# Eleven up-projection pairs of the second FFN as seven block products instead of eight

## The chip, the core and the metric

The kernel runs on one core of a Trainium2 chip. The metric is the device time of one launch in microseconds; the time of a kernel is the median of its runs. A core has five engines with queues of their own, each worked off strictly in order: TensorE (PE; its weight loads are PEld), VectorE (DVE), ScalarE (ACT), GpSimd (POOL) and SyncE (SP). Transfers are issued from SP's and POOL's queues. Engines wait for each other, and for transfers, on semaphores.

## What is computed

Two layers of a decoder trunk with 512 tokens, 16 meta tokens ahead of them (L = 528), a width of 1024 and an FFN width of 2816:

```python
for l in range(DEPTH):                      # DEPTH = 2
    h = mixer_sublayer(h, ...)              # attention, conformer conv and short conv groups
    h = ffn_sublayer(h, ...)
return h[:, N_META:]

def ffn_sublayer(h, pre_g, post_g, w_up, conv_w, w_down):
    u = rms_norm(h, pre_g)
    z = jnp.einsum("bld,df->blf", u, w_up)
    z = causal_depthwise_conv(z, conv_w)    # 3 taps
    g, up = jnp.split(z, 2, axis=-1)
    y = jnp.einsum("blf,fd->bld", jax.nn.silu(g) * up, w_down)
    return h + rms_norm(y, post_g)
```

Everything is float32.

## The kernel before

Channels lie on the 128 partitions, tokens along the free axis; a [1024, 528] activation is eight tiles of 128 x 528. A float32 product is made of three products in a rounded format: operands are split into a high part (a cast on ScalarE) and a low part (the rest, a subtraction on VectorE), and `mm3` (L706) issues high x high, high x low and low x high for every 128 rows k and every half of the tokens.

Weights lie in DRAM in the order of their use, in chunks of up to 128 x 1024. Each is loaded by SP into one of three `raw` buffers, cast into `whi` and subtracted into `wlo`. `next_w` hands out the next chunk and prepares two ahead; in the mixers and at the seams a planner (`Flow`) sets the order by hand, in the FFN loops the program order and a list scheduler do, on the simulated readiness of each instruction.

The FFN runs in three parts of 8, 7 and 7 pairs (`PARTS`). A pair f is a gate tile f and an up tile 22 + f of 128 channels. For each of the two, eight k, three products and two token halves are accumulated in a pair of PSUM banks (48 matmuls), VectorE multiplies the result by the token norm `rz` into one of four z buffers (`scaled`, L1988, its products on L1992 and L1995), and `ffn_gate` (L2031) applies the three taps, SiLU and the product and splits g into `yhi` and `ylo`. The input u is so far not normalised; `uhi` and `ulo` hold h times the gain. After each part eight down products add up in `yp`. The last layer needs only 514 columns of z (250 and 264 in the two halves) and 512 of the output.

GpSimd does little: memsets of constants and padding at the start; in each mixer memsets of `cxp`, `vals`, `fx`, `k` and `q`, then `dm` (L1483) and the causal selects of the probabilities (L1526). In the first layer's FFN it also issues twelve transfers `w_split` (L545), which store split weights of the second layer. Transfers issued by POOL share eight completion semaphores (lanes, DMASW0 to DMASW7): each waits for the one that last used its lane, that is the one eight before it.

Of the kernel before, what the change touches and what calls it, by code (L numbers as in the profile page):

```python
# [2 lines left out]

# [6 lines left out]
F32 = mybir.dt.float32  # L10
F32R = mybir.dt.float32r
# [4 lines left out]
P = 128  # L16
D = 1024
KD = D // P
L = 528
# [6 lines left out]
DFF = 2816  # L26
NF = DFF // P
PARTS = (8, 7, 7)
AHEAD = 2
CHUNK = 1056  # L30

# [77 lines left out]
def chunk_cols(c):  # L109
    return sum(n for _, n in c[4])  # L110
# [269 lines left out]
def tile_hybrid_trunk(ctx: ExitStack, tc: tile.TileContext, xT, wflat, pv_d, out):  # L380
# [80 lines left out]
    def const_col(name, val):  # L461
        t = T(const, [P, 1], F32, name)
        nc.gpsimd.memset(t, val)
        return t

    c_one = const_col("c_one", 1.0)
    c_eps = {RMS_EPS: const_col("c_rms", RMS_EPS), LN_EPS: const_col("c_ln", LN_EPS)}

    EXPSET = "natural_log_exp_and_others"
    nc.scalar.preload_act_table_set(EXPSET)  # L470
# [33 lines left out]
    wx = [None]  # L504


    pw_place = [None]

    def wtile(i, tag):
# [4 lines left out]
            return pw_place[0][:, :n] if tag == "whi" else pw_place[0][:, n:2 * n]  # L514
        return T(wx[0], [P, WCHUNK], F32R, tag) if i in wide else T(wp, [P, CHUNK], F32R, tag)

    def prep_one():
        i = wpos[0]
        if i >= len(chunks):
            return  # L520
# [6 lines left out]
        nc.scalar.copy(hi[:, :sz], raw[:, :sz])  # L527
        nc.vector.tensor_sub(lo[:, :sz], raw[:, :sz], hi[:, :sz].bitcast(F32))  # L528
        ready.append((i, tuple(t[:, :sz].rearrange("p (k n) -> p k n", n=n) for t in (hi, lo))))
# [1344 lines left out]
    wxs = wide_pool("wx0")  # L1874
# [77 lines left out]
    for l in range(DEPTH):  # L1952
# [14 lines left out]

        with ms, tc.manual_schedule(engines=every):
            flow.yields = YM
            y, y_at, early = mixer(l, ypool, first, wxs.close, i_spans, front, rzs, u_at)  # L1970
        ms, front, u_at = ExitStack(), None, {}
        wxs = wide_pool(f"wy{l}", [early.slot[hf] for hf in range(2)], early.third)

        with tc.tile_pool(name=f"fp{l}", bufs=2, reuse_waits="tile") as fp:
            hp = wxs.enter_context(tc.tile_pool(name=f"hg{l}", bufs=1, side="right", reuse_waits="tile"))
            rz, yp = T(hp, [P, L], F32, "rz"), T(hp, [P, KD, L], F32, "yp")

            def u_in(b, k, hf):
# [1 line left out]
                return (uhi, ulo)[b][:, k, a:z]  # L1980


            zs = [T(fp, [P, 2 + L], F32, f"z{i}", 1) for i in range(4)]
            if off:
                for t in zs:
                    nc.gpsimd.memset(t[:, :off], 0.0)
# [45 lines left out]
            def ffn_gate(f):  # L2032
# [15 lines left out]
                nc.vector.tensor_sub(glo, cs[0], ghi.bitcast(F32))  # L2048
                return ghi, glo

            g = {}
            f0 = 0
            for part, nf in enumerate(PARTS):
                for f in range(f0, f0 + nf):
                    for i in (2 * f, 2 * f + 1):
# [6 lines left out]
                        ps = mmt()  # L2062
                        mm3({hf: ps[:, hf, :iws[hf]] for hf in range(2)}, w, range(KD), u_in)
                        scaled(i, [ps[:, :, :H]] if i0 == 0 else [ps[:, hf, :iws[hf]] for hf in range(2)])
                    g[f] = ffn_gate(f)
                ks = list(range(nf))
                grhs = lambda b, k, hf, f0=f0: g[f0 + k][b][:, fw * hf:fw * (hf + 1)]
                if part < len(PARTS) - 1:
                    for m in range(KD):
                        w = next_w()  # L2070
                        ps = mmt()
                        if final:

                            mm3({0: ps[:, 0, :2 * fw]}, w, ks, lambda b, k, hf, f0=f0: g[f0 + k][b][:, :2 * fw])
                            d, src = yp[:, m, t0:], ps[:, 0, :2 * fw]
                        else:
                            mm3({hf: ps[:, hf, :fw] for hf in range(2)}, w, ks, grhs)
                            d, src = two(yp[:, m, t0:]), ps[:, :, :fw]
                        if part == 0:
                            nc.scalar.copy(d, src)  # L2080
                        else:
                            nc.vector.tensor_add(d, d, src)  # L2082
                        if l == 0 and m%2:
                            store_one()
                else:
                    gpre = None if final else pvs[l + 1][1][:, _COLS["mix_pre_g"]:]
                    first = raw = rzs = None
                    if not final:
                        raw = [[g[f0 + k][b] for k in range(nf)] + [T(ypool, [P, L], F32R, f"y{n}{nf}")] for b, n in enumerate(("hi", "lo"))]
                        raw = [[[t[:, half_sl(hf)] for t in ts] for ts in raw] if hf < 2 else None for hf in range(2)]  # L2090
                        rzs = [rz[:, half_sl(hf)] if raw[hf] else None for hf in range(2)]
                        first = First(lambda b, k, hf, raw=raw: raw[hf][b][k] if raw[hf] else u_rhs(b, k, hf), [H, H], {})
                    with tc.manual_schedule(engines=every):
                        plan_begins()
                        norms.factors([rs, zs[0][:, 2:]], h=APART)
                        flow.yields = YE
                        if not final:
                            plan_w(after_down, WE)
                        plan_w(len(chunks) if final else after_mixer[l + 1])
                        t_last = [Tok(flow.now + 7.5)]  # L2100
                        finish(norms, h, {}, o_spans, ks, grhs, lambda k, nf=nf: t_last if k == nf - 1 else [], yp,
                               gains("ffn_post_g"), gpre, SPLIT["ffn_w_down"], first, raw=raw, rzs=rzs, u_at=u_at)
                f0 += nf
        if final:
            wxs.close()


# [47 lines left out]
```

## Time and profile before

| | us |
|---|---|
| three runs | 1293.91, 1294.2, 1294.4; median 1294.2 |
| span of the profiled execution | 1292.0 (2.2 less than the median of the runs) |
| TensorE busy | 1274.1 (99%) |
| VectorE busy | 864.3 (67%) |
| ScalarE busy | 618.1 (48%) |
| GpSimd busy | 103.1 (8%) |

The first mixer runs from the start to about 215 us. In the second layer's FFN the down product of part 0 begins at about 994 us, that of part 1 at about 1117, and the last up pair ends at about 1237. A busy time is a share over stages with different limits; what bounds a stage is read from the row of that stage, and from the chain of waits, which follows the last instruction back to what released it. In a row of the groups the columns are line, engine, operation, output and inputs, shapes, count, then busy us and mean ns of one, then idle time just before and what ended it.

### The profile page before, as it was taken

What the parts mean: (1) busy time and instruction counts of PE and PEld (TensorE: products, weight loads), DVE (VectorE), ACT (ScalarE), POOL (GpSimd) and SP (SyncE); (2) the same over time, 40 slices, a digit from 0 to 9 for tenths busy, and PEclk for the clock granted to TensorE, in tenths of its full rate; (3) what the DMA queues carried; (4) which work ended last, traced back from release to release, by engine and by line L of the source; (5) the groups of instructions that cost most, each with busy time, mean ns of one, the idle gap of its engine ahead of it and who ended that gap; (6) DMA issues with size and microseconds to landing.
All of it is one profiled execution on the core that took longest, in us unless ns stands there. A gap on an engine that the chain in (4) does not pass through costs nothing. (4 is left out here: it accounts for less than half of the span.)

```text
span 1292.0 us, 24062 instructions
## 1 busy us (share of the span) xinstructions
PE 1274.1 (99%) x9802; PEld 1223.7 (95%) x9802; DVE 864.3 (67%) x1477; ACT 618.1 (48%) x1157; POOL 103.1 (8%) x266
## 2 busy tenths in 40 slices
PE   8999999999999999999999999999999999999997
PEld 8999899999999999999999998899999799989997
DVE  7888775687634664567688877757776257637664
ACT  7255577654433342334672555865543333313443
POOL 1313311000000000000003232100000000000000
PEclk9999999999999999999999999999999999999999
DMA  7136133502273225223541452344132332232221
GB/s 239 34 101 159 50 100 103 178 18 98 89 235 134 99 87 179 95 96 101 177 170 36 113 144 62 89 135 129 34 99 82 98 98 84 72 123 85 90 72 65
DMA packets 50094, 137.35 MB, mean 106 GB/s; under 512 B 6000, under 2 KB 16368, under 8 KB 49984
## 3 DMA queue, kind: packets, MB, share of 16 engines
q1 hardware_dynamic: 48208, 129.39, 32.0%
q0 software_dynamic: 1776, 6.42, 1.3%
q8 instruction: 77, 1.26, 0.4%
q14 instruction: 33, 0.27, 0.1%
HBM read 114.33 MB, written 10.62 MB: 97 GB/s over the span
## 5 line engine op out<-in xcount | busy, mean ns | idle before, releaser
L712 PE MATMUL psum<-uhi,whi 128*128 128x264 f32 (+1 forms) x1840 | 426.0, 287 | 1.6 <-ACT uhi L1927 0.8
L712 PE MATMUL psum<-ulo,whi 128*128 128x264 f32 (+1 forms) x1840 | 420.8, 284 | 0.6 <-DVE ulo L1929 0.4
L712 PE MATMUL psum<-uhi,wlo 128*128 128x264 f32 (+1 forms) x1840 | 418.8, 283 | 0.0
L712 PEld LDWEIGHTS psum<-uhi,whi 128*128 128x128 f32 x1840 | 304.9, 188 | 6.1 <-issue 1.6
L712 PEld LDWEIGHTS psum<-ulo,whi 128*128 128x128 f32 x1840 | 305.9, 189 | 1.4 <-DVE ulo L1929 0.6
L712 PEld LDWEIGHTS psum<-uhi,wlo 128*128 128x128 f32 x1840 | 305.6, 189 | 0.0
L712 PE MATMUL psum<-yhi,whi 128*128 128x264 f32 (+3 forms) x984 | 275.8, 301 | 2.4 <-ACT yp L2080 1.0
L712 PE MATMUL psum<-yhi,wlo 128*128 128x264 f32 (+3 forms) x984 | 272.9, 297 | 1.1 <-DVE wlo L668 1.1
L712 PE MATMUL psum<-ylo,whi 128*128 128x264 f32 (+3 forms) x984 | 272.3, 297 | 0.0
L527 ACT CAST whi<-raw 128x1024 fp32r<-128x1024 f32 (+1 forms) x110 | 113.2, 1031 | 195.8 <-PE psum L712 186.4
L712 PEld LDWEIGHTS psum<-yhi,whi 128*128 128x128 f32 x984 | 177.0, 188 | 10.4 <-ACT yp L2080 1.6
L712 PEld LDWEIGHTS psum<-yhi,wlo 128*128 128x128 f32 x984 | 177.3, 188 | 6.8 <-DVE wlo L668 1.5
L712 PEld LDWEIGHTS psum<-ylo,whi 128*128 128x128 f32 x984 | 177.4, 188 | 5.5
L528 DVE TENSOR_TENSOR wlo<-raw,whi 128x1024 fp32r<-128x1024 f32 (+1 forms) x110 | 131.9, 1200 | 67.7 <-ACT whi L527 65.6
L2029 DVE SCALAR_TENSOR_TENSOR c<-z,pv,c 128x528 f32<-128x528 f32 (+1 forms) x176 | 131.9, 756 | 2.7
L668 DVE TENSOR_TENSOR wlo<-raw,whi 128x1024 fp32r<-128x1024 f32 (+2 forms) x80 | 95.5, 1203 | 30.1 <-ACT whi L664 29.6
L664 ACT CAST whi<-raw 128x1024 fp32r<-128x1024 f32 (+2 forms) x80 | 81.8, 1030 | 25.6 <-PE psum L712 17.9
L1028 DVE SCALAR_TENSOR_TENSOR cacc<-apad,pv,cacc 128x528 f32<-128x528 f32 x120 | 87.6, 771 | 0.1
L2047 ACT CAST yhi<-c 128x528 fp32r<-128x528 f32 (+1 forms) x44 | 27.6, 627 | 108.8 <-DVE c L2043 108.7
L2039 ACT ACTIVATE c<-c 128x528 f32<-128x528 f32 (+1 forms) x44 | 28.1, 639 | 79.4 <-DVE c L2029 79.4
L1992 DVE TENSOR_TENSOR z<-psum,rz 128x528 f32<-128x528 f32 x40 | 28.3, 708 | 53.7 <-PE psum L712 52.2
L2027 ACT ACTIVATE c<-z,pv 128x528 f32<-128x528 f32 (+1 forms) x88 | 63.4, 727 | 0.1
(221 smaller groups left out, 1455.9 us busy)
## 6 DMA issues: line engine op xcount, KB each, us to landing
raw<-in_w_dram SPq DMA_DIRECT2D x160, 512.0 KB
raw<-in_w_dram SPq DMA_DIRECT2D x32, 448.0 KB
h<-in_x_dram SPq DMA_DIRECT2D x16, 264.0 KB
q<-pair_hi SPq DMA_DIRECT2D x24, 132.0 KB
k<-pair_hi SPq DMA_DIRECT2D x24, 132.0 KB
w_split<-whi POOLq DMA_DIRECT2D x6, 512.0 KB, 3.4
w_split<-wlo POOLq DMA_DIRECT2D x6, 512.0 KB, 7.1
whi<-w_split SPq DMA_DIRECT2D x6, 512.0 KB
```

Source lines behind the costliest of these rows:

```text
L527: nc.scalar.copy(hi[:, :sz], raw[:, :sz])
L528: nc.vector.tensor_sub(lo[:, :sz], raw[:, :sz], hi[:, :sz].bitcast(F32))
L664: nc.scalar.copy(box["hi"][:, :sz], box["raw"][:, :sz])
L668: nc.vector.tensor_sub(lo[:, :sz], box["raw"][:, :sz], box["hi"][:, :sz].bitcast(F32))
L712: nc.tensor.matmul(d, lhsT=w[a][:, k, cols], rhs=rhs(b, k, hf), start=start and i == 0 and p == 0, stop=stop and i == n - 1 and p == 2)
L1028: nc.vector.scalar_tensor_tensor(conv[j], in0=src, in1=conv[j], scalar=col("a_dw_w", CK * j + i), op0=ALU.mult, op1=ALU.add)
L1992: nc.vector.tensor_mul(two(t[:, off:]), srcs[0], two(rz))
L2027: nc.scalar.activation(dst, src[:, 2:2 + 2 * fw], AF.Copy, scale=wtap(2, t))
L2029: nc.vector.scalar_tensor_tensor(dst, in0=src[:, i:i + 2 * fw], scalar=wtap(i, t), in1=dst, op0=ALU.mult, op1=ALU.add)
L2039: silu = nc.scalar.activation(cs[0], cs[0], AF.Silu)
L2047: nc.scalar.copy(ghi, cs[0])
```

## The change

In the second layer, the pairs f = 8, 9, 10, 12 to 17, 19 and 20 (`SEVEN`) are made by Strassen's scheme in Winograd's form. The 2 x 2 blocks are, on the weights' side, gate and up by the two halves of k (512 rows each), and on the other side u by the halves of k and two spans of 258 tokens, which overlap by two columns. Seven products of 4 k x 3 parts are issued instead of eight.

- **Weight sums.** For each pair, `sum_steps` makes two arrays `c` and `b` of 128 x 1024 in DRAM: eight transfers of 128 x 512 issued by GpSimd, four that copy and four that accumulate (`accum_op` add). The generator is called two steps per pair of the first layer's FFN: 88 transfers in all.
- **Loads.** Instead of the up chunk, `prep_one` loads `c`, `b` and the second half of up (`d`), and splits all three: 128 x 1024, 128 x 1024 and 128 x 512. The parts of `c` have one buffer (`chi`, `clo`), those of `d` sit in the tiles `yhi7` and `ylo7`.
- **The input.** `normalised` builds a normalised u (32 VectorE operations), four sums of its blocks `t0` to `t3`, and splits these and u again, spread over pairs 3 to 7 and the down product of part 0. Pairs 11, 18 and 21, made as before, then need no factor `rz`, and ScalarE copies their results.
- **The products.** `seven_pair` uses three PSUM banks, alternately 0 to 2 and 3 to 5. ScalarE writes the negated first block into the second bank, on which the next product accumulates, and copies intermediate sums out while the banks go on; VectorE subtracts twice. The last product of a pair is issued inside the next one. The other products of these parts use the banks 6, 7 and 2, 3.
- The pool of wide weight tiles is closed while `c` and the sums live, and opened again for the last down product. Three constant columns share one tile.

```diff
+SEVEN = {1: (8, 9, 10, 12, 13, 14, 15, 16, 17, 19, 20)}
+K2 = KD // 2
+SB = K2 * P
...
+    def sum_steps(l, f):
+
+        gate, up = (flat_w(up_chunk[l, t]) for t in (f, NF + f))
+        c, b = (T(dram, [P, 2 * SB], F32, f"w_sum_{n}{l}_{f}") for n in "cb")
+        sums[l, f] = c, b
+        x, y = slice(0, SB), slice(SB, 2 * SB)
+
+        def put(to, src, add=False):
+            nc.gpsimd.dma_start(to, src, **({"accum_op": ALU.add} if add else {}))
+
+        put(c[:, x], up[:, x])
+        put(b[:, y], up[:, x])
+        put(b[:, x], gate[:, x])
+        put(c[:, y], gate[:, y])
+        yield
+        put(c[:, x], up[:, y], True)
+        put(b[:, y], gate[:, x], True)
+        yield
+        put(b[:, x], c[:, x], True)
+        yield
+        put(c[:, y], b[:, x], True)
+        yield
...
+        if i in seven_up:
+            if not parts:
+                c, b = sums[seven_up[i]]
+                parts.extend((("c", c), ("b", b), ("d", flat_w(i)[:, SB:])))
+            kind, src = parts.popleft()
+            wpos[0] += not parts
+            raw = T(wp, [P, CHUNK], F32, "raw", 3)
+            sz = src.shape[-1]
+            nc.sync.dma_start(raw[:, :sz], src)
+            if kind == "c":
+                hi, lo = (T(tx[0], [P, 2 * SB], F32R, t) for t in ("chi", "clo"))
+            elif kind == "b":
+                hi, lo = (T(wp, [P, CHUNK], F32R, t) for t in ("whi", "wlo"))
+            else:
+                hi, lo = (T(ypool, [P, L], F32R, f"y{t}{max(PARTS) - 1}") for t in ("hi", "lo"))
+            nc.scalar.copy(hi[:, :sz], raw[:, :sz])
+            nc.vector.tensor_sub(lo[:, :sz], raw[:, :sz], hi[:, :sz].bitcast(F32))
...
+            def product(bank, w, k0, rhs, start, stop):
+
+                for k in range(K2):
+                    for p, (a, b) in enumerate(((0, 0), (0, 1), (1, 0))):
+                        nc.tensor.matmul(psum[:, bank, :n7], lhsT=w[a][:, k0 + k, :], rhs=rhs(b, k),
...
+            def seven_pair(f):
...
+                w = next_w()
+                product(x, w, 0, u(0, h7[0]), True, False)
+                nc.scalar.activation(by, bx, AF.Copy, scale=-1.0)
+                wc = next_w()
+                product(z, wc, 0, t(0), True, False)
+                tmp = T(fp, [P, 2, H], F32, "acc", 2)[:, 0, :n7]
+                nc.scalar.copy(tmp, bz)
+                finish_pair()
+                wb = next_w()
+                product(y, wb, 0, t(1), False, False)
+                nc.scalar.copy(gate[:, hi], by[:, skip:])
+                product(x, w, K2, u(K2, h7[0]), False, True)
+                nc.scalar.copy(gate[:, lo], bx)
+                product(z, wc, K2, u(K2, h7[1]), False, True)
+                nc.vector.tensor_sub(gate[:, hi], bz[:, skip:], gate[:, hi])
+                product(y, wb, K2, t(2), False, False)
+                nc.scalar.copy(up[:, hi], by[:, skip:])
+                nc.vector.tensor_sub(up[:, hi], up[:, hi], tmp[:, skip:])
+                wd = next_w()
+
+                def rest():
+                    product(y, wd, 0, t(3), False, True)
+                    nc.scalar.copy(up[:, lo], by)
+                    g[f] = ffn_gate(f)
+
+                late_ups.append(rest)
...
             for part, nf in enumerate(PARTS):
                 for f in range(f0, f0 + nf):
+                    if l + 1 in SEVEN:
+                        for _ in range(2):
+                            next(todo, None)
+                    if f in seven:
+                        seven_pair(f)
+                        continue
+                    finish_pair()
+                    if seven and f == 2:
+                        building[0] = normalised()
+                    if 2 < f < 8:
+                        build(5)
```

The scheduler moves the transfers. On GpSimd's queue, from the opening into the first layer's mixer, these rows follow each other before (hsel is a constant of the opening, cxp, vals, fx and k are tiles of the mixer):

```order
L459 MEMSET hsel_13_98 64x64 [waits Pool_49]
L1078 MEMSET cxp_683 128x2 [waits DVE_49,Pool_49]
L437 MEMSET vals_694 128x528 [waits PE_49]
L437 MEMSET vals_694 128x40x2 [waits Pool_49]
L1217 MEMSET fx_697 128x40
```

In the changed kernel, on the same queue, from the last constant on; w_sum_c_8 is the array c of pair 8, and the name in brackets the semaphore waited for:

```order
L465 MEMSET hsel_13_98 64x64 [waits Pool_49]
L528 DMA w_sum_c_8_405_3553<-in_w_dram 128x512 [waits DMASW2_49]
...
L528 DMA w_sum_b_16_582_5603<-in_w_dram 128x512 [waits DMASW3_49]
L1136 MEMSET cxp_681 128x2 [waits DVE_49,Pool_49]
...
L443 MEMSET vals_692 128x528 [waits PE_49]
L528 DMA w_sum_c_20_682_6793<-in_w_dram 128x512 [waits DMASW7_49]
...
L528 DMA w_sum_b_16_582_5603<-w_sum_c_16_581_5602 128x512 [waits DMASW3_49]
L443 MEMSET vals_692 128x40x2 [waits Pool_49]
L1275 MEMSET fx_695 128x40
```

None of the 88 transfers stands in the first FFN. 4 stand among the constants, 17 ahead of the last of them, 59 ahead of the memset of cxp, 62 ahead of that of vals, 75 ahead of that of fx. The rest, with the last memsets before dm:

```order
L443 MEMSET k_92_707 64x528 [waits Pool_49]
L528 DMA w_sum_c_16_581_5602<-w_sum_b_16_582_5603 128x512 [waits DMASW4_49]
L528 DMA w_sum_c_17_638_6277<-w_sum_b_17_639_6278 128x512 [waits DMASW6_49,DMASW5_49]
L528 DMA w_sum_c_19_660_6535<-w_sum_b_19_661_6536 128x512 [waits DMASW0_49]
L528 DMA w_sum_b_20_683_6794<-w_sum_c_20_682_6793 128x512 [waits DMASW7_49,DMASW2_49]
L443 MEMSET k_92_707 1x528 [waits Pool_49]
L443 MEMSET q_100_715 32x528 [waits PE_49]
...
L528 DMA w_sum_c_20_682_6793<-w_sum_b_20_683_6794 128x512 [waits DMASW7_49,DMASW1_49]
L443 MEMSET k_96_711 1x528 [waits Pool_49]
...
L443 MEMSET dm_108_739 128x16 [waits PE_49,Pool_49]
```

All 88 stand ahead of dm, and 44 of them accumulate. In the second FFN, VectorE's queue in part 1 has for one pair before (z are the four buffers, c the taps' tiles):

```order
L1995 TENSOR_TENSOR z_1023_10059<-psum_67,rz_10055 128x250
L1995 TENSOR_TENSOR z_1023_10059<-psum_67,rz_10055 128x264
L528 TENSOR_TENSOR wlo_12490<-raw_12487,whi_12489 128x1024
L2029 SCALAR_TENSOR_TENSOR c_12543<-z_1023_10059,pv_4_72,c_12543 128x512 x2
```

(the gate half of it), and after, around pair 13:

```order
L576 TENSOR_TENSOR clo_12573<-raw_12570,chi_12572 128x1024
L2114 TENSOR_TENSOR ylo_1248_12469<-c_12458,yhi_1247_12468 128x512
L2239 TENSOR_TENSOR zs_10162<-psum_67,zs_10162 128x256
L576 TENSOR_TENSOR wlo_12579<-raw_12576,whi_12578 128x1024
L2095 SCALAR_TENSOR_TENSOR c_12628<-zs_10162,pv_4_72,c_12628 128x512 x2
L586 TENSOR_TENSOR wlo_12645<-raw_12642,whi_12644 128x1024
L2242 TENSOR_TENSOR zs_10162<-zs_10162,acc_12509 128x256
L576 TENSOR_TENSOR ylo_1267_12598<-raw_12595,yhi_1266_12597 128x512
```

Three full low weight parts and a half one (clo, wlo, wlo, and ylo of d) stand where a pair had two, and the two products with rz have become two subtractions of 256 columns.

More of the change, by code (lines that the diff above doesn't have):

```diff
@@ L2 @@
 from contextlib import ExitStack
+from itertools import chain
 import concourse.bass as bass
@@ L515, in wtile @@
         return T(wx[0], [P, WCHUNK], F32R, tag) if i in wide else T(wp, [P, CHUNK], F32R, tag)
+    parts = deque()
     def prep_one():
@@ new lines, in tile_hybrid_trunk, with build @@
+            ts, n_seven, primed = [], [0], set()
+            building = [None]
+            def build(n=None):
+                while building[0] is not None and (n is None or n > 0):
+                    try:
+                        op = next(building[0])
+                    except StopIteration:
+                        building[0] = None
+                        return
+                    if op is None:
+                        if n is not None:
+                            return
+                        continue
+                    op()
+                    if n is not None:
+                        n -= 1
@@ L2085, in tile_hybrid_trunk @@
                 else:
+                    if seven:
+                        pools.pop().close()
+                        pools.append(ExitStack())
+                        wx[0] = pools[1].enter_context(tc.tile_pool(name=f"wz{l}", bufs=WIDE, side="right", reuse_waits="tile"))
                     gpre = None if final else pvs[l + 1][1][:, _COLS["mix_pre_g"]:]
@@ L2104, in tile_hybrid_trunk @@
         if final:
-            wxs.close()
+            close_pools()
 def kernel(**inputs):
```

118 lines of the change are left out of this document (105 added, 13 removed).

## The prediction

> **What bounds the kernel now.** I read the page's busy shares first, then the chain of waits, then the stages that the change touches.
>
> ```profile
> span 1292.0 us, 24062 instructions
> PE 1274.1 (99%) x9802; PEld 1223.7 (95%) x9802; DVE 864.3 (67%) x1477; ACT 618.1 (48%) x1157; POOL 103.1 (8%) x266
> ...
> 1003.29 123.41 PE psum L712 x856
> 1126.70 0.02 issue
> 1126.72 0.70 DVE yp L2082
> 1127.42 0.04 issue
> 1127.47 119.19 PE psum L712 x876
> ```
>
> TensorE has no gaps: 99% of the span, and in the second layer's FFN the chain is one run of matmuls, broken once by 0.70 us. So there every matmul removed is worth its issue interval, and anywhere every microsecond for which TensorE has nothing to do is lost. Two stretches matter: the up products of the second FFN, where matmuls go, and the first 160 us, at whose head the new transfers stand in the built order. The rows of the windows view (busy us per engine, granted clock, DMA share of 16 engines, GB/s):
>
> ```profile
> 0.00:10.00 10.00, 8.04 (x51) 7.82 (x52) 3.82 (x8) 5.13 (x10) 3.86 (x26) 1.00 0.82 288
> 10.00:20.00 10.00, 9.02 (x69) 8.51 (x68) 8.95 (x14) 8.63 (x15) 0.00 (x0) 1.00 0.89 309
> 20.00:30.00 10.00, 10.00 (x80) 9.76 (x79) 8.77 (x18) 7.93 (x16) 0.00 (x0) 1.00 0.55 174
> 30.00:60.00 30.00, 28.80 (x234) 28.50 (x234) 26.39 (x50) 9.12 (x18) 11.32 (x26) 1.00 0.11 37
> 1040.00:1118.00 78.00, 78.00 (x651) 77.86 (x650) 52.65 (x79) 30.51 (x40) 0.00 (x0) 1.00 0.29 91
> ```
>
> The last row is nearly seven up pairs of the second FFN: 78.00 / 651 = 0.120 us per matmul of 250 or 264 columns at full clock, VectorE at 67%. The first rows show DMA engines that are nearly full for 20 us.
>
> **The gain: eleven pairs.** A pair has 96 matmuls now and 84 after (seven block products of 4 x 3), of 258 columns, close to the 257 of the mean. 12 x 0.120 = 1.44 us, less a trifle for the wider column count: 1.40 us a pair, 15.4 us for eleven.
>
> **What may hold it back.** VectorE and ScalarE get more to do per pair. Durations of the forms in that stage, and of a ScalarE copy out of PSUM:
>
> ```profile
> L2029 DVE SCALAR_TENSOR_TENSOR c<-z,pv,c 128x512 f32<-128x512 f32 x26 | 19.5, 749 | 0.5
> L528 DVE TENSOR_TENSOR wlo<-raw,whi 128x1024 fp32r<-128x1024 f32 x11 | 13.5, 1225 | 2.8 <-ACT whi L527 2.8
> L527 ACT CAST whi<-raw 128x1024 fp32r<-128x1024 f32 x11 | 11.6, 1053 | 13.6 <-PE psum L712 13.6
> L2027 ACT ACTIVATE c<-z,pv 128x512 f32<-128x512 f32 x13 | 9.4, 721 | 0.0
> L1995 DVE TENSOR_TENSOR z<-psum,rz 128x264 f32<-128x264 f32 x14 | 5.9, 423 | 0.0
> L2039 ACT ACTIVATE c<-c 128x512 f32<-128x512 f32 x7 | 4.4, 632 | 14.7 <-DVE c L2029 14.7
> L2048 DVE TENSOR_TENSOR ylo<-c,yhi 128x512 fp32r<-128x512 f32 x6 | 4.2, 692 | 4.1 <-ACT yhi L2047 4.1
> L1753 ACT ACTIVATE yp<-psum,pg 128x250 f32<-128x250 f32 x8 | 3.8, 472 | 6.6 <-PE psum L712 6.6
> ```
>
> VectorE per new pair: three low parts of 1024 columns (3 x 1.225), one of 512 (0.692), two subtractions of 256 (2 x 0.42), four taps (4 x 0.749), the gate product and the low part of g (2 x 0.69): 9.6 us. ScalarE: 3 x 1.053, about 0.6 for the half cast, six copies of 258 columns (6 x 0.47), two taps (2 x 0.721), SiLU and cast of g (2 x 0.63): 9.3 us. TensorE: 84 x 0.120 = 10.1 us. Both stay under it by 5 to 8%, but they now hand results to TensorE within a pair (the negated block, a bank that must be copied before it is accumulated on), so a late cast is a stall. In part 0, pairs 6 and 7 also build the sums of u: about 4 to 5 VectorE operations of 1032 columns each, some 5 us on top of some 8 against 11.5 us of TensorE, 3.4 us late in all. I take 5 us lost (3.4 and 0.15 per pair); the bounds are 0 and the whole 15.4. The extra loads, 1.75 instead of 1 MB a pair, find a DMA share of 0.29 and cost nothing; if that cover were gone a pair would wait some 2 us. The wide weight pool opened late has the 11.5 us of pair 21 to hide in.
>
> **The loss: 88 transfers ahead of the first mixer's GpSimd work.** They are written in the loop of the first FFN, but depend on no computed tile, and in the built order they stand at the head of POOL's queue: 59 before the memset of cxp, 75 before that of fx, 87 before the second memset of k, all 88 before dm. Each waits for the lane of the one eight before it, so POOL moves on only as the transfers land. Behind the waiting instruction are memsets that in the trace of before ran early:
>
> ```profile
> 3.33 0.20 POOL L977 MEMSET apad<- 128x30 f32 x2
> ...
> 45.15 0.10 POOL L1078 MEMSET cxp<- 128x2 f32 x1 [39.90 <-DVE apad L995]
> 46.22 0.13 POOL L1217 MEMSET fx<- 128x40 f32 x1
> 47.74 1.12 POOL L437 MEMSET k<- 64x528 f32 x2
> 57.63 0.17 POOL L437 MEMSET dm<- 128x16 f32 x2
> 81.14 0.73 POOL L1483 TENSOR_SCALAR dm<-ident,mcol 16x16 fp32r<-16x16 f32 x2 [23.35 <-DVE mcol L1475]
> ```
>
> and these first need them (VectorE's fx, and SP's transfer into k, without which the first scores cannot be formed):
>
> ```profile
> 52.79 0.17 DVE L1271 TENSOR_TENSOR fx<-psum,pv 128x8 f32<-128x8 f32 x1 [0.90 <-ACT vals L1267]
> ...
> 74.70 0.55 SPq L574 DMA_DIRECT2D k<-sq  x1
> ```
>
> Queues are in order: VectorE stuck at fx issues no low weight parts, and TensorE stops. Now the price of a transfer. No row shows a copy from DRAM to DRAM or an accumulating one. The queue rows give the engines' rate, the other the issue:
>
> ```profile
> q1 hardware_dynamic: 48208, 129.39, 32.0%
> ...
> L545 POOL DMA_DIRECT2D w_split<-whi x6: 531/531/600, 353.6 to 498.5; - x6
> ...
> DMA to landing us min/median/max: 3.3/5.9/8.0
> ```
>
> 129.39 MB / (0.320 x 1292.0 us) = 313 GB/s of full engines; 128 x 512 x 4 B = 262 KB take 0.84 us in one pass. Below: 0.75 us for every one (288 / 0.82 = 351 GB/s, the first window). Above: two passes for a plain copy (reads and writes the same memory, 1.68) and three for an accumulating one (two reads, a write, 2.51). Nothing decides between the ends, so I take the middle: 1.26 and 1.68. 44 x 1.26 + 44 x 1.68 = 129 us; bounds 66 and 184. Issue alone, 88 x 0.531 = 47 us, is below all of these and hides behind them.
>
> The same engines carry the loads of the opening: 8.2 + 8.9 + 5.5 + 0.11 x 30 = 25.9 us of full engines. The sums start at 3.5 us, behind apad. The second memset of k comes when 87 are issued and all but about five have landed: 3.5 + 129 x 83/88 + 25.9 + 0.5 = 152 us, against 74.70: 77 us late. The memsets from there to dm take the 9 us that they took before (48.3 to 57.6), so dm is free at 161, wanted at 81 + 77 = 158: 80 us in all. The gate at fx comes earlier (67 landed, about 125 against 53, 72 late) and lies inside this. The late first weights and h lie inside it too, since POOL's time is absolute. Bounds by the same steps: 20 and 132 us. TensorE restarts at a lower speed after a stop; the warm-up shows its price:
>
> ```profile
> L1892 PE MATMUL psum<-warm 128*128 128x264 f32 x44 | 7.1, 333 | 1.3 <-DVE warm L1890 1.3
> ```
>
> 44 in 7.1 us is 0.161 each, 44 x 0.041 = 1.8 us more than at speed; two or three stops, 4 us.
>
> The Trainium skill, "DMA: Bandwidth & Descriptors", section "Anatomy of one DMA", gives a GpSimd-issued transfer 2.0 us plus its bytes at 436 GB/s. By that 512 KB take 3.2 us, and the trace's shortest landing, 3.3, agrees. With eight in flight the fixed part would hide and 88 would need 53 us, which with the steps above is an estimate of 8 us of delay and about 1292 us in all. The same page, section "Latency and other measured facts", has DRAM-to-DRAM copies at 207 to 214 GB/s per direction, 1.23 to 1.27 us for one of these; by that the sum stays as it is. No run here shows either for such a copy.
>
> **Sum** against the profiled execution: 1292.0 + 80 + 4 - 15.4 + 5 = 1365.6 us; the median of the runs is 2.2 above the span: 1368 us.
>
> **Rivals.**
> 1. The transfers take one pass each, accumulating or not (0.84): 74 us. For it: the engines overlap reads and writes when they load SBUF. Against: an accumulating copy has a second input. k is then ready at 3.5 + 70 + 25.9 + 0.5 = 100, 25 late, dm 28. 1294.2 + 28 + 4 - 10.4 = 1316 us.
> 2. POOL is not late (the faster side): transfers are taken as fast as they are issued, 87 x 0.531 + 3.5 = 50 us plus a few for memsets, before 74.70. Decides if a transfer with its share of the loads costs under 0.7 us. For it: POOL idles 40 us before cxp and 23 before dm. Against: the opening's loads alone fill 26 us of engines. 1294.2 - 15.4 + 5 = 1284 us.
> 3. The delay comes and the second FFN gains nothing, because VectorE and ScalarE, at 92 to 95% of a pair with hand-offs, hold it at 11.5 us: the 10.4 (15.4 - 5) are gone, 1368 + 10.4 = 1378 us. For it: low weight parts are issued between hand-offs. Against: their busy sums are under TensorE's.
> 4. The page's 436 GB/s, worked as a mechanism of this queue: delay 8 us, which the gain of 10.4 cancels: 1292 us.
> 5. An accumulating transfer is worse than three passes: above 1430 us.
>
> **How the numbers follow.** Forecast 0.50; rivals 0.20, 0.07, 0.16, 0.03, 0.04. 1368 is the forecast's time. The low end, 1294.2 + 20 - 15.4 = 1299, is the cheapest transfer by the rows with the full gain; the high end, 1294.2 + 132 + 4 = 1430, the dearest with no gain. A measurement here tells about 0.2% (2.6 us) from no change. Faster by more: rival 2 and a little of 4, 0.08. Within: the rest of 4, 0.03. Slower: 0.89.
>
> **What would show it.** Right: on POOL's timeline dm's first use moves from 81 us to about 160; idle time of VectorE before fx and of TensorE in the first 160 us, about 80 us, released by POOL; a clock below full just after; the packets of q0 up by 23 MB and more. In the second FFN 84 matmuls a pair, and the stretch from the end of part 0's down product to the start of the last one shorter by about 15 us or, with stalls, 10. Wrong: POOL reaches dm before 85 us, or TensorE stays at 99% of the span in the first 160 us; or TensorE waits for casts in the seven pairs by more than 1 us each.

## The result

The changed kernel takes 1348.6 us (median of four runs, 1346.2 to 1351.7) against 1294.3 (1293.9 to 1294.4): a ratio of 1.042, interval [1.041, 1.044]. The forecast was 1368 with a range of 1299 to 1430. The profiled execution took 1351.7 us with a span of 1350.0, 58.0 longer than the span before; it is the longest of the four, so the profile shows some 3 us more than the median.

The page of the changed kernel (busy us and shares, then tenths in 40 slices of 33.75 us, then the queue that GpSimd's transfers use):

```profile
span 1350.0 us, 24094 instructions
...
PE 1277.8 (95%) x9672; PEld 1223.4 (91%) x9672; DVE 887.6 (66%) x1493; ACT 667.2 (49%) x1265; POOL 164.9 (12%) x354
...
PE   5748899999999999999999999999989999989997
...
PEclk8879899999999999999999999999989999999999
DMA  9998333260225522522362143316112235434421
...
q0 software_dynamic: 11632, 29.50, 8.8%
```

TensorE now has 130 matmuls fewer (11 x 12, less two that prepare banks) and yet is busy 3.7 us longer, because part of them ran at a lower clock. Its holes lie in the first five slices, the DMA engines are full in the first three, and there are two dents much later, in the 30th and the 36th. Queue q0 moved 23.1 MB more.

**The opening.** Waits of TensorE over 3 us in the first 150 us of the changed kernel (timeline of PE; start, duration, work, and in brackets the idle time before it and what ended it):

```profile
37.82 2.10 PE L907 MATMUL psum<-acc,om_d 128*128 128x264 f32 x4 [16.23 <-DVE acc L867]
...
55.44 0.39 PE L770 MATMUL psum<-uhi,whi 128*128 128x264 f32 x1 [3.50 <-ACT uhi L1991]
...
101.08 0.59 PE L1340 MATMUL psum<-whi,uhi 128*128 128x264 f32 x1 [16.90 <-DVE fx L1329]
...
127.80 0.34 PE L1526 MATMUL psum<-k,q 128*16 128x16 f32 x2 [3.92 <-DMA k<-sq]
...
138.36 1.28 PE L1550 MATMUL psum<-dm,ones_r 128*128 128x264 f32 x2 [3.29 <-POOL dm L1541]
```

The first two of them are not GpSimd's. VectorE's sum was late because ScalarE stood still, and ScalarE waited for the first weights. Before the second, ScalarE waited for weights once more, and the steps of the norm and the casts of u stood behind that cast (timeline of ACT):

```profile
34.75 1.04 ACT L722 CAST whi<-raw 128x1024 fp32r<-128x1024 f32 x1 [16.78 <-DMA raw<-in_w_dram]
...
47.80 1.07 ACT L722 CAST whi<-raw 128x1056 fp32r<-128x1056 f32 x1 [5.20 <-DMA raw<-in_w_dram]
```

TensorE had almost nothing to do for 20 us, in which the DMA engines were full, and again from 90 to 100 us (windows: the length, then busy us and count of PE, PEld, DVE, ACT and POOL, granted clock, DMA share, GB/s):

```profile
20.00:30.00 10.00, 1.59 (x14) 1.37 (x12) 0.00 (x0) 0.00 (x0) 4.51 (x8) 0.78 1.04 270
30.00:40.00 10.00, 2.18 (x6) 1.80 (x7) 4.07 (x5) 4.12 (x6) 3.82 (x6) 0.50 1.03 324
...
90.00:100.00 10.00, 0.00 (x0) 0.00 (x0) 0.00 (x0) 0.00 (x0) 6.21 (x9) 0.50 1.10 221
```

The last three are GpSimd's. Its timeline, with the memsets that stand behind transfers, the last transfer and the first use of dm:

```profile
80.43 0.11 POOL L1136 MEMSET cxp<- 128x2 f32 x1
...
100.39 0.43 POOL L1275 MEMSET fx<- 128x40 f32 x1
...
120.07 0.54 POOL L443 MEMSET k<- 1x528 f32 x1
...
130.22 0.81 POOL L528 DMA_DIRECT2D w_sum_c<-w_sum_b  x1 [5.57 <-DMA w_sum_b<-w_sum_c]
...
135.31 3.69 POOL L1541 TENSOR_SCALAR dm<-ident,mcol 16x16 fp32r<-16x16 f32 x5
```

The memset of fx ran at 100.39 instead of 46.22, the last transfer went out at 130.22, and dm was first used at 135.31 instead of 81.14, 54.2 us late. A landmark behind all of it, GpSimd's next memset of cxp, moved from 161.71 to 218.77: the opening cost 57.1 us.

**The second FFN.** The remaining 58.0 - 57.1 = 0.9 us are all that the later stages add: the eleven pairs brought nothing. The waits of TensorE there, of 0.12 us and more, from pair 2 to the end of the up pairs:

```profile
996.01 0.55 PE L770 MATMUL psum<-uhi,whi 128*128 128x250 f32 x1 [4.97 <-DVE zs L2061]
...
1068.71 0.50 PE L770 MATMUL psum<-yhi,whi 128*128 128x512 f32 x1 [0.97 <-ACT yp L2303]
...
1113.64 0.51 PE L2201 MATMUL psum<-t,yhi 128*128 128x258 f32 x2 [0.65 <-ACT zs L2241]
...
1124.06 0.51 PE L2201 MATMUL psum<-t,chi 128*128 128x258 f32 x2 [0.30 <-ACT chi L575]
...
1166.55 0.51 PE L2201 MATMUL psum<-t,yhi 128*128 128x258 f32 x2 [0.29 <-ACT zs L2241]
...
1189.23 0.91 PE L770 MATMUL psum<-yhi,whi 128*128 128x512 f32 x2 [4.17 <-ACT yhi L2113]
```

The wait of 0.97 us stood there before as well. The waits inside the seven-product pairs (those for t) make 1.24 us in all; the two large waits lie at the seams. The first is VectorE's: as soon as the norm rz is known, it makes the 16 pieces of the normalised u in one go, 6.43 us, and the taps and low weight parts that pair 2 and the following need come after (timeline of DVE):

```profile
979.03 0.77 DVE L2067 TENSOR_TENSOR zs<-psum,rz 128x264 f32<-128x264 f32 x2
979.72 6.43 DVE L2138 SCALAR_TENSOR_TENSOR yp<-h,pg,rz 128x256 f32<-128x256 f32 x16
986.07 0.76 DVE L2067 TENSOR_TENSOR zs<-psum,rz 128x264 f32<-128x264 f32 x2
...
989.02 4.05 DVE L2095 SCALAR_TENSOR_TENSOR c<-zs,pv,c 128x512 f32<-128x512 f32 x6
...
995.46 1.07 DVE L2061 TENSOR_TENSOR zs<-psum,rz 128x250 f32<-128x250 f32 x3
```

In the program these 16 (not 32, as the text on the change has it; with the sums and splits there are 28) are called five per pair from pair 3 on; the list scheduler took them as early as their inputs allow. The second is the end of part 1. Pair 14 is a seven-product pair, and its last product is issued when the pair is over; from its last matmul at 1184.78 the rest of the down product has to wait for a whole gate (timeline of ACT: copy, first tap, and after VectorE's taps and product the cast of g):

```profile
1185.10 0.37 ACT L2247 COPY zs<-psum 128x258 f32<-128x258 f32 x1 [4.74 <-PE psum L2201]
1185.50 0.72 ACT L2093 ACTIVATE c<-zs,pv 128x512 f32<-128x512 f32 x1
1188.56 0.62 ACT L2113 CAST yhi<-c 128x512 fp32r<-128x512 f32 x1 [2.33 <-DVE c L2109]
```

After each of them TensorE restarts slowly (windows around the first wait):

```profile
990.00:995.00 5.00, 1.04 (x9) 0.84 (x7) 5.00 (x8) 3.05 (x4) 0.00 (x0) 1.00 0.43 163
995.00:1000.00 5.00, 3.99 (x19) 4.02 (x20) 5.00 (x11) 2.92 (x5) 0.00 (x0) 0.51 0.36 105
1000.00:1005.00 5.00, 5.00 (x36) 5.00 (x36) 3.85 (x7) 1.78 (x3) 0.00 (x0) 0.81 0.00 0
```

Matmul by matmul, the starts are twice as far apart at first (timeline of PE, behind either wait):

```profile
996.36 0.41 PE L770 MATMUL psum<-ulo,whi 128*128 128x250 f32 x1
996.57 0.41 PE L770 MATMUL psum<-uhi,wlo 128*128 128x250 f32 x1
...
1002.18 0.28 PE L770 MATMUL psum<-ulo,whi 128*128 128x264 f32 x1
1002.30 0.28 PE L770 MATMUL psum<-uhi,wlo 128*128 128x264 f32 x1
...
1190.55 0.63 PE L770 MATMUL psum<-yhi,wlo 128*128 128x512 f32 x1
1190.97 0.63 PE L770 MATMUL psum<-ylo,whi 128*128 128x512 f32 x1
...
1193.24 0.39 PE L770 MATMUL psum<-yhi,whi 128*128 128x512 f32 x1
1193.47 0.39 PE L770 MATMUL psum<-ylo,whi 128*128 128x512 f32 x1
```

Counted singly, 30 matmuls start between 996.01 and 1002.30, in 6.3 us instead of 30 x 0.120 = 3.6: 2.7 us lost. Between 1189.23 and 1193.47 there are ten, in 4.2 us; those of 512 columns that follow start every 0.232 us, so 2.3 would have done: 1.9 us lost. Together 4.97 + 4.17 + 1.24 of waits and 2.7 + 1.9 of slow restarts make 15.0 us, nearly the 15.4 us that the pairs were to save.

### The profile page after: what moved, and what is told of

Its sections match the earlier page's. It is cut to its first block, busy times and chain, and to the rows that moved or that the text cites. A ratio compares the mean times of both kernels' runs of the same rounds, so it can differ in the third digit from the quotient of the medians.

```text
span 1350.0 us, 24094 instructions
## 1 busy us (share of the span) xinstructions
PE 1277.8 (95%) x9672; PEld 1223.4 (91%) x9672; DVE 887.6 (66%) x1493; ACT 667.2 (49%) x1265; POOL 164.9 (12%) x354
## 5 line engine op out<-in xcount | busy, mean ns | idle before, releaser
L770 PE MATMUL psum<-uhi,whi 128*128 128x264 f32 (+1 forms) x1488 | 358.2, 290 | 9.2 <-DVE zs L2061 5.0
L770 PE MATMUL psum<-ulo,whi 128*128 128x264 f32 (+1 forms) x1488 | 352.4, 286 | 0.6 <-DVE ulo L1993 0.4
L770 PE MATMUL psum<-uhi,wlo 128*128 128x264 f32 (+1 forms) x1488 | 351.8, 286 | 0.0
L770 PEld LDWEIGHTS psum<-uhi,whi 128*128 128x128 f32 x1488 | 253.6, 191 | 13.8 <-ACT c L2105 5.1
L770 PEld LDWEIGHTS psum<-ulo,whi 128*128 128x128 f32 x1488 | 254.0, 191 | 1.3 <-DVE ulo L1993 0.6
L770 PEld LDWEIGHTS psum<-uhi,wlo 128*128 128x128 f32 x1488 | 253.9, 191 | 0.0
L770 PEld LDWEIGHTS psum<-yhi,whi 128*128 128x128 f32 x984 | 178.5, 190 | 16.5 <-ACT yhi L2113 4.4
L2095 DVE SCALAR_TENSOR_TENSOR c<-zs,pv,c 128x528 f32<-128x528 f32 (+1 forms) x176 | 131.8, 757 | 12.0 <-ACT c L2093 9.7
L2093 ACT ACTIVATE c<-zs,pv 128x528 f32<-128x528 f32 (+1 forms) x88 | 63.5, 728 | 3.5 <-DVE zs L2239 1.9
L2058 DVE TENSOR_TENSOR zs<-psum,rz 128x528 f32<-128x528 f32 x40 | 28.3, 708 | 53.7 <-PE psum L770 52.1
L1340 PE MATMUL psum<-whi,uhi 128*128 128x264 f32 (+3 forms) x160 | 46.9, 293 | 16.9 <-DVE fx L1329 16.9
```

The source lines that it names most:

```text
L770: nc.tensor.matmul(d, lhsT=w[a][:, k, cols], rhs=rhs(b, k, hf), start=start and i == 0 and p == 0, stop=stop and i == n - 1 and p == 2)
L1340: nc.tensor.matmul(ps[:n, :nw], lhsT=(uhi, ulo)[ui][:, k, P * b:P * b + n], rhs=w[wi][:, k % 4, :], start=k == 0 and p == 0, stop=k == KD ...
L2058: nc.vector.tensor_mul(two(t[:, off:]), srcs[0], two(rz))
L2093: nc.scalar.activation(dst, src[:, 2:2 + 2 * fw], AF.Copy, scale=wtap(2, t))
L2095: nc.vector.scalar_tensor_tensor(dst, in0=src[:, i:i + 2 * fw], scalar=wtap(i, t), in1=dst, op0=ALU.mult, op1=ALU.add)
```

## The experiments

Two questions were open: whether the opening's loss is GpSimd's late queue or the DMA engines taken from the first loads, and what the pairs are worth alone.

**Sums alone.** The kernel before, with the transfers issued as in the change, and nothing that reads them:

```diff
+                    if l + 1 in SEVEN:
+                        for _ in range(2):
+                            next(todo, None)
```

> The kernel before plus the 88 transfers alone (same generator, called at the same place; nothing reads the sums, all pairs stay ordinary). Theory (the whole loss comes from the transfers at the head of GpSimd's queue, and the seven-product pairs are worth about nothing): 1294.3 + 57 = 1351 us, within 4. Rival (the seven-product pairs keep their 10 us of gain, and the transfers cost more than 57): 1359 or more. Other rival (the stages around the pairs lose time, the transfers cost less): below 1342.

1347.6 us against 1294.1, ratio 1.041 [1.039, 1.043]: 53.5 us, at the lower edge of the theory's range (1347 to 1355). The transfers are all of the loss as far as these runs can tell: the change's own 54.3 us are 0.8 more, and the single runs of either kernel lie 5 to 7 us apart. The run without sums, below, measures the rest of the edit by itself.

**Twenty-four transfers.** The same with three pairs.

```diff
-SEVEN = {1: (8, 9, 10, 12, 13, 14, 15, 16, 17, 19, 20)}
+SEVEN = {1: (8, 9, 10)}
```

> The kernel before plus 24 transfers (three pairs) instead of 88. They issue and land within about 24 x 1.2 + 20 us of other loads, so GpSimd reaches the memset of cxp at about 50 us against 45. Theory (GpSimd's queue is what is late): at most 8 us of loss, 1294 to 1302 us, TensorE's idle time released by GpSimd or not there. Rival (the transfers take the DMA engines from the first weight loads): the 16 us idle stretch at 20 to 36 us stays, with a cold restart, 1310 to 1314 us, and TensorE waits for casts that wait for raw.

1314.7 us, ratio 1.016 [1.014, 1.017]: 20.5 us, just over the rival's upper end, and its mechanism is the one seen. GpSimd issued its last sum at 41.41 and then waited 24 us for somebody else; TensorE's long wait is the one of the first weights (timelines of POOL and of PE):

```profile
41.41 0.81 POOL L528 DMA_DIRECT2D w_sum_c<-w_sum_b  x1 [0.81 <-DMA w_sum_b<-w_sum_c]
...
66.36 0.10 POOL L1115 MEMSET cxp<- 128x2 f32 x1 [24.13 <-DVE apad L1032]
```

```profile
37.52 2.10 PE L886 MATMUL psum<-acc,om_d 128*128 128x264 f32 x4 [13.49 <-DVE acc L846]
```

So there is a first loss of about 20 us that has nothing to do with GpSimd's queue. Whether it adds to the queue's delay or lies inside it was to be shown with six pairs, and with all 88 transfers started later.

**Forty-eight transfers**, `SEVEN = {1: (8, 9, 10, 12, 13, 14)}`:

> The kernel before plus 48 transfers (six pairs). From the profiles of the runs so far a plain transfer takes 0.81 us of full engines and an accumulating one 1.51, so GpSimd is through them at 3.5 + 24 x 0.81 + 24 x 1.51 + 26 = 85 us and reaches dm at about 95. With 24 transfers dm was used at 102 (the first loads are late in any case). Theory (the larger of the two delays counts, not the sum): about as much as with 24, 1314 to 1320 us. Rival (loss in proportion to the transfers, or the two delays add): 48/88 x 54 = 29 or 20 + 14, 1323 to 1328 us.

1319.8 us, ratio 1.020 [1.019, 1.022]: 25.8 us, 5.3 more than with 24, inside the range for the larger of the two delays though at its upper edge, and under what a sum or a proportion gives. The last transfer went out at 75.39, and dm's first use, at 106.67, waited for VectorE and not for the queue. The 5.3 us more are late weights too: TensorE waited 15.90 us where it waited 13.49 with 24, and then 3.35 where ScalarE's next load was late, 5.8 more in all.

**A late start.** The changed kernel with its transfers behind GpSimd's memset of cxp:

```diff
-            nc.gpsimd.memset(cx[:, :2], 0.0)
+            behind.append(nc.gpsimd.memset(cx[:, :2], 0.0))
...
-                        for _ in range(2):
-                            next(todo, None)
+                        with tc.issue_after(behind[0].ins):
+                            for _ in range(2):
+                                next(todo, None)
```

> The changed kernel with the transfers held back until the memset of cxp (45 us), so that the loads of the opening have the DMA engines to themselves; 49 of them then stand ahead of the second memset of k, 87 ahead of the first use of dm. Theory (GpSimd's queue in absolute time sets the end of the opening): 45.3 + 87 x 1.16 + 10 us of other loads + 9 us of memsets = 165 us for dm against 81, so 84 us late and 1294 + 84 + 3 + 1 = 1382 us, 1365 to 1395, although the transfers collide with fewer loads. Rival (the collision of the transfers with the first loads is what counts, 20 of the 57 us): 1330 us.

1367.0 us, ratio 1.056 [1.055, 1.058]: 18 us slower than the change, in the lower part of the theory's range and far from the rival. The wait for the first weights is gone, and the three behind GpSimd's queue come to 63.3 us instead of 24.1 (timeline of PE; VectorE's fx in the first row stood behind the memset of fx):

```profile
72.35 0.59 PE L1341 MATMUL psum<-whi,uhi 128*128 128x264 f32 x1 [14.13 <-DVE fx L1330]
...
110.44 0.51 PE L1527 MATMUL psum<-k,q 128*16 128x16 f32 x2 [15.25 <-POOL q L443]
...
152.90 1.25 PE L1551 MATMUL psum<-dm,ones_r 128*128 128x264 f32 x2 [33.92 <-POOL dm L1542]
```

So GpSimd's time counts in absolute terms: what starts later ends later. It is not the whole shift, though: the first transfer went out at 45.73 instead of 3.44, 42 us later, and dm was used 16.5 us later, and why the shift is so much smaller was not traced. The size was off, 73 us instead of 88: dm was used at 151.8, not at 165.

**Plain copies.** All 88 without the accumulation:

```diff
-            nc.gpsimd.dma_start(to, src, **({"accum_op": ALU.add} if add else {}))
+            nc.gpsimd.dma_start(to, src, **({}))
```

> The changed kernel with all 88 transfers plain copies (the sums are not formed, so the weights of the products are not the sums; the shapes of the work are the same). Forecast as it was on record (1.26 us plain, 1.68 accumulating): 44 x 0.42 = 18 us less of lag, 1330 us. Theory from the trace (the windows with accumulating transfers alone move 205 GB/s, 1.28 us each, and all 88 took 1.16 us each in the mean, so a plain one is near 1.0): 44 x 0.24 = 11 us less, 1338 us. Rival (both kinds cost the same): 1348 us. One pass for a plain copy (0.84): 1329 us.

1322.3 us, ratio 1.022 [1.020, 1.024], below all four. The queue's row of the page:

```profile
q0 software_dynamic: 8816, 29.50, 6.7%
```

Before, q0 took 1.3% of 1292.0 = 16.8 us of full engines for its few transfers. Here it took 6.7% of 1319.9 = 88.4, so a plain copy costs (88.4 - 16.8) / 88 = 0.81 us. In the changed kernel 8.8% of 1350.0 = 118.8, so the 44 accumulating ones cost (118.8 - 16.8 - 44 x 0.81) / 44 = 1.51 us each. The runs with 24 and 48 transfers agree: their q0 took 3.3% of 1313.7 and 5.6% of 1318.0, less 16.8 that is 26.6 and 57.0 us, against 27.8 and 55.7 by these prices. The time fell by 26.3 us, less than 44 x 0.70 = 31; the loss of the first weights remains, which fits: TensorE waited 17.27 us for them here too, and 2.65 at most for anything else.

**The pairs without sums.** The changed kernel without any transfer, with loads of the same size from the up and gate chunks in place of c and b:

```diff
-                c, b = sums[seven_up[i]]
+                b, c = (flat_w(up_chunk[seven_up[i][0], t + seven_up[i][1]]) for t in (0, NF))
...
-                        for _ in range(2):
-                            next(todo, None)
+                        pass
```

> The changed kernel without any transfer: c and b are loaded from the up and the gate chunk instead of the sums (so the weights of the products are not the sums, the work and its shapes are the same). Theory: the second FFN's own worth is -1 to -3 us, so 1291 to 1293. Forecast as it was on record (the pairs gain 10.4): 1284. Rival (nothing gained): 1294 and more. Against the run with the sums in the first FFN, the difference is what 88 transfers cost there: 0 to 2 by the theory.

1295.1 us, ratio 1.0007 [0.9998, 1.0017]: 0.9 over the kernel before, the line of the rival that nothing is gained; the theory's 1291 to 1293 was 2 us too low. The two waits are there without any transfer (timeline of PE):

```profile
938.78 0.35 PE L770 MATMUL psum<-uhi,whi 128*128 128x250 f32 x1 [4.25 <-DVE zs L2061]
...
1131.74 1.22 PE L770 MATMUL psum<-yhi,whi 128*128 128x512 f32 x2 [4.17 <-ACT yhi L2113]
```

**Sums in the first FFN.** A one-column copy on GpSimd that reads the pair's z buffer holds the transfers back:

```diff
+                marks = T(fp, [P, NF], F32, "marks", 1)
...
-                        for _ in range(2):
-                            next(todo, None)
+                        mark = nc.gpsimd.tensor_copy(marks[:, f:f + 1], zs[(2 * f) % len(zs)][:, 2:3])
+                        with tc.issue_after(mark.ins):
+                            for _ in range(2):
+                                next(todo, None)
```

> The changed kernel with each pair of steps of the transfers pinned behind a one-column copy by GpSimd that reads a z buffer of the running pair of the first FFN, so that they go out there. Theory: the opening is as before, and the second FFN as in the changed kernel, 1350.0 - 57 = 1292 us, 1290 to 1295. Rival (the transfers cost where they go now too, since loads, stores and sums share the DMA engines): 1300 or more, with TensorE waiting for casts in the first FFN. Rival (the pairs were held by something that the late opening caused): below 1287.

1296.3 us, ratio 1.002 [1.001, 1.003], between the theory's 1290 to 1295 and the rival's 1300. The opening is back to what it was, and the transfers cost about 1.2 us against the run without them, which their intervals hardly tell apart. The next four runs start from this kernel and mend the seams.

**Pair 14 ordinary instead of pair 11:**

```diff
-SEVEN = {1: (8, 9, 10, 12, 13, 14, 15, 16, 17, 19, 20)}
+SEVEN = {1: (8, 9, 10, 11, 12, 13, 15, 16, 17, 19, 20)}
```

> The kernel with the sums in the first FFN, and pair 14, the last of part 1, made as an ordinary pair instead of pair 11 (still eleven seven-product pairs). Theory (the last product of a seven-product pair leaves its whole gate, taps, SiLU, product and cast, ahead of the down product): the 4.17 us wait for yhi at the end of part 1 goes to under 1 us, and the slow restart after it, 1 to 2 us, with it: 1296.3 - 5 = 1291 us, 1289 to 1293. Rival (the wait is caused by VectorE's and ScalarE's load in these pairs, not by the order): 1295 to 1297.

1289.1 us, ratio 0.996 [0.995, 0.998]: 7.2 us off, more than the 5 expected; the wait of 4.17 us and the restart after it, which had cost 1.6 us in the run that it starts from (counted as above), make 5.8, and the restart at the first seam cost 1.9 here instead of 2.8. The wait at that place is 0.31 us, the one for VectorE's yp that the kernel before has there too.

**The normalised input spread over the pairs**, behind the z products (`last` is the latest of them):

```diff
+            last = [None]
...
-                    nc.vector.tensor_mul(t[:, off + a - i0:off + z - i0], src, rz[:, a:z])
+                    last[0] = nc.vector.tensor_mul(t[:, off + a - i0:off + z - i0], src, rz[:, a:z])
...
-                    if 2 < f < 8:
-                        build(5)
+                    if 2 < f < 8:
+                        n_ops = (8, 8, 2, 3, 3)[f - 3]
+                        if seven:
+                            with tc.issue_after(last[0].ins):
+                                build(n_ops)
```

> The kernel with the sums in the first FFN, and the operations that build the normalised input pinned behind the z products of the pair before (8, 8, 2, 3 and 3 per pair from pair 3 on), so that VectorE does not do all 16 products with rz at once. Theory: the 4.98 us wait of TensorE for VectorE's zs in part 0 goes, with a slow restart of some 2 us: 1296.3 - 7 = 1289 us, 1288 to 1292. Rival (VectorE has no room in part 0, the wait moves to later pairs): 1294 to 1298, with TensorE waiting for zs or for a cast in pairs 4 to 7.

1290.8 us, ratio 0.997 [0.996, 0.998]: 5.5 us off, inside the range. VectorE had the room; two waits of 0.55 and 0.43 us at the start of part 0's down product came in place of the 4.98, and the wait of 4.16 us at the end of part 1 is still there, with a restart that cost 2.7 us in this run.

**Both:**

> Both edits. Theory (two waits at the seams of the second FFN are what eats the 15.4 us of the seven-product pairs): 1296.3 - 5 - 7 = 1284 us, 1282 to 1287, under the kernel before by 10. Rival (one hides behind the other): 1289 and more.

1284.6 us, ratio 0.993 [0.991, 0.994]: 9.5 us under the kernel before and 64 under the change. The largest waits that are left in the second FFN, beside the 0.97 us that was always there (timeline of PE):

```profile
993.73 0.49 PE L770 MATMUL psum<-yhi,whi 128*128 128x512 f32 x1 [0.55 <-ACT whi L585]
...
1062.24 0.51 PE L2203 MATMUL psum<-t,chi 128*128 128x258 f32 x2 [0.46 <-ACT chi L575]
...
1174.92 0.51 PE L2203 MATMUL psum<-t,chi 128*128 128x258 f32 x2 [0.45 <-ACT chi L575]
```

**A twelfth pair**, 18, with three steps of sums per pair of the first FFN:

> The kernel with both seams mended, with pair 18 as a twelfth seven-product pair (three steps of transfers per pair of the first FFN, to have them all in time). Theory: 12 matmuls less, 1284.6 - 1.4 = 1283.2 us, 1282.5 to 1284.5. Rival (six such pairs in a row leave VectorE and ScalarE, or the three raw buffers, no ordinary pair to catch up in): 1285 and more, with TensorE waiting for chi in part 2.

1285.2 us, ratio 0.994 [0.993, 0.996], with runs from 1284.3 to 1291.4. The interval overlaps that of eleven pairs ([0.991, 0.994]): nothing can be told of the 1.4 us. The wait for chi grew to 0.90 us, in part 1 and not in part 2.

The opening of each kernel, as the medians and the timelines of POOL show it:

| kernel | loss in us, of the median | dm first used | next memset of cxp |
|---|---|---|---|
| before | | 81.1 | 161.7 |
| 24 transfers | 20.5 | 102.4 | 182.9 |
| 48 transfers | 25.8 | 106.7 | 187.3 |
| 88 plain, with the pairs | 28.2 | 108.0 | 188.0 |
| 88, alone | 53.5 | 132.1 | 214.8 |
| the change | 54.3 | 135.3 | 218.8 |
| the change, late start | 73.0 | 151.8 | 232.1 |

## Why the prediction was right, and where it was not

**GpSimd's queue (right; the price too high).** The memsets of cxp, fx and k and the first use of dm stood behind the transfers, and VectorE, SP and TensorE behind those, as forecast. The term of 80 us measured 54.2. The sign that TensorE stands idle for about 80 us behind GpSimd did not show: its waits there come to 24.1 us, and 19.7 more are for weights, inside the same delay. The wrong factor of the term is the price of a transfer: 1.26 us plain and 1.68 accumulating were taken as the middle between bounds, and the runs gave 0.81 and 1.51, 102 us for all instead of 129. With 102 in the prediction's own step, k's second memset comes at 3.5 + 102 x 83/88 + 25.9 + 0.5 = 126 us and dm is free at 135; the trace has 120.07 and 135.31. That the second agrees is partly luck: from k to dm the queue took 15.2 us where the forecast had 9, and k came 6 earlier. The lower bound for every transfer, one pass, was right for the plain copies (rival 1 with half its condition); an accumulating one takes 1.8 of the forecast's passes of 0.84. The Trainium skill, "DMA: Bandwidth & Descriptors", "Latency and other measured facts", puts copies from DRAM to DRAM, in tiles of 128 x 16 KiB issued from other queues, at 207 and 214 GB/s per direction at the two best of its row pitches; here 262 KB in 0.81 us are 324 GB/s for a plain one, and in 1.51 us 174 for an accumulating one, and the measurement decides.

**The late first weights (right here, and more than said).** The prediction counted them as inside the queue's delay, since that runs in absolute time. The late start shows that this holds for 88 transfers. The prediction gave them no price of their own; 24 transfers show about 20 us and 48 about 26, which is what stays when GpSimd is through in time, and so rival 2 (GpSimd not late, 1284 us) could not have come out at its price.

**Slow restarts in the opening (the size not shown).** 4 us were expected. Behind the first use of dm 2.9 more are lost (57.1 - 54.2), and the granted clock was 0.67 from 135.3 to 144.0 us and 0.94 in the 10 us after. But these 2.9 are a difference of two landmarks and no measured restart: with the late start the same stretch, from dm to the memset of cxp, takes 80.3 us against 80.6 before, although the clock was 0.69 from 151.8 to 161.0, behind a wait of 33.92. The two restarts in the second FFN cost 2.7 and 1.9 where the warm-up row had given 1.8. The Trainium skill, "TensorE: Matmul & The Clock Gate", "Part 1: The HAM clock gate", has the clock at half after an idle window of about 3.4 us and for about as long; the trace agrees in kind (0.51 in the 5 us after a wait of 4.97), and takes somewhat longer (starts 0.21 to 0.22 us apart for 5.9 us).

**The gain of the pairs (right, and all given back).** With both seams mended the stretch from the 0.31 us wait in part 1's down product to TensorE's 0.96 us wait in the last norm takes 146.8 us (1124.85 to 1271.61) against 153.2 before (1127.47 to 1280.68): 6.4 less for five pairs, with a wait of 0.45 us for chi in it, near the 7.0 of 1.40 each. The stalls were put at 5 us, 3.4 for the build (two pairs of 5 + 8 - 11.5 us make 3.0) and 0.15 a pair. Per pair that was right: 1.24 us in eleven. The build's term was too small, and it was put in the wrong place: not 5 operations on top of pairs 6 and 7, but 16 in one block ahead of pair 2's z products, since the scheduler does not keep the program's spreading; 4.97 us of wait and 2.7 of restart. And the end of part 1 was not in the sum at all: pair 14's gate, 4.17 and 1.9. The prediction named pair 21 as cover for the wide pool and did not ask which pair closes part 1. So the span has 15.4 - 16.3 in place of 15.4 - 5; of the 16.3, the rows show 15.0.

**The sum.** Against 1365.6 us for the profiled execution: 25.8 too much for the queue, 1.1 for what follows dm, 11.3 too little for the second FFN, which makes 1350.0. The errors have opposite signs, and that the total came nearer than the queue's term is luck.

**Rival 3 (nothing gained in the second FFN)** came true in its result and not in its mechanism: VectorE and ScalarE do not hold a pair at 11.5 us, since with both seams mended the pairs save 9.5 us net, and without a change to the work on either engine. The extra loads cost next to nothing, as said: TensorE waited 0.30 us once for chi. Rivals 4 and 5 fell with the prices.

**What is open.** From 1284.6 to the 1278.7 of the full gain 5.9 us are left; small waits of TensorE (2.2 us in all) and the transfers in the first FFN (about 1.2) are seen, the other 2.5 were not traced.

## What to carry to other kernels

A transfer that depends on no computed tile can be put wherever the scheduler finds an idle queue, here at the start: what matters is not where the loop stands in the code but what comes behind it in that queue and which loads it meets. Tie such work to a tile of the stage where it belongs. When a stage is made shorter for the bound engine, look first at its two ends, at what has to be ready when it begins and what is still to be finished when it ends: a gain of 12 matmuls per pair was lost in two waits outside the pairs.

## What the hardware showed that was not expected

An accumulating transfer from DRAM to DRAM took 1.51 us of full engines for 128 x 512 float32, 1.9 times a plain one (0.81); a plain one costs no more than one pass. And a wait of TensorE of 4 to 5 us cost 1.6 to 2.8 us more in the slow restart behind it, and not the same each time: behind the same wait of 4.17 us at the end of part 1 the losses, counted as above, were 1.9 us in the change, 1.6 with the sums in the first FFN and 2.7 without sums.
